# Up projection of a hybrid decoder layer: seven products in three PSUM banks, pairs interleaved, one subtraction moved from POOL to VectorE

## Chip, cores and metric

One core of one Trainium2 chip. The metric is the device time of one execution in microseconds (us); the median of three runs of the kernel before is 2045.83 us (2045.69 to 2045.98). TensorE (PE) multiplies, VectorE (DVE), ScalarE (ACT) and GpSimd (POOL) work on tiles in SBUF and PSUM, SyncE (SP) issues the DMAs.

## What is computed

One decoder layer: two token mixers (a Mamba-2 branch and windowed attention), their gated sum, a layer norm, a convolutional feed-forward block and a second layer norm. The change lies in the feed-forward block, of which the reference is

```
def conv_ffn(h, w_up, conv_w, conv_b, w_down):
    u = causal_depthwise_conv(jnp.einsum('bsd,df->bsf', h, w_up), conv_w, conv_b)
    gate, val = jnp.split(u, 2, axis=-1)
    return jnp.einsum('bsf,fd->bsd', jax.nn.silu(gate) * val, w_down)
```

with 1024 positions, h of 1024 channels, 2816 gate channels and as many value channels, and three taps in the convolution. All is float32.

## The kernel before

A float32 product is made of three products of rounded parts: a tile is split into a high part (`hi`, rounded by ScalarE, L100) and a low part (`lo`, the difference, L101, on the engine that the caller names), and hi x hi, hi x lo and lo x hi are summed.

**The up projection.** It runs in 22 *pairs* f = 0 to 21; a pair is 128 gate channels and the 128 value channels that belong to them, for all 1024 positions. The pair is computed as a 2 x 2 block product by Winograd's scheme with seven instead of eight block products. The rows of the blocks are gate and value weights, their columns the two halves of the 1024 input channels: A11, A12 are the halves of the gate weights (`uraw`, with parts `uhi` and `ulo`, made in `pair_first`), A21, A22 those of the value weights (`raw1`). On the other side stand the transposed activations, B11, B21, B22 (with their parts `hh`, `hl`) and the combinations T1 to T4, which are made once. `pair_s` loads `raw1` (L747) and makes four combinations S1 to S4 of the weights (L751 to L754) on POOL, except for pair 0, where it is VectorE, and splits each into `sh` (ScalarE) and `sl` (POOL). `pair` splits A22 into `a22h` and `a22l`, the second on POOL too.

The products are p1 = A11 B11, p2 = A12 B21, p3 = S4 B22, p4 = A22 T4, p5 = S1 T1, p6 = S2 T2, p7 = S3 T3. `prod` (L719 to L726) makes one of them from 12 matmuls of 128 x 128 by 128 x 512 (L724), so a pair has 84 and the stage 1848. Every product has a PSUM bank of its own: `bank` hands out six with the tag "b" and two with the tag "h".

`pair` then puts the four quarters of the result together on VectorE: cg (gate) has p1 + p2 in its first half, cv (value) and the second half of cg come from u2 = p1 + p6, u2 + p7, and p5, p4, p3. ScalarE copies p1 to SBUF (L903); VectorE does seven adds, each with one operand from SBUF and one from PSUM (L906, L907, L910, L912, L915, L916, L919). `gated` (L921) takes both through the convolution (`conv`: one ScalarE operation L126 and two VectorE steps L128 that read and write SBUF), applies silu (L122 on ScalarE, L123 on VectorE), multiplies (L926) and stores the result to DRAM (`asc`, L928). cg, cv, hg, hv and a scratch tile are five [128, 1024] tiles `cs` with one buffer each; `raw1` and S1 to S4 have one buffer each, `sh` and `sl` four.

**What sets the order.** A scheduler that simulates the program orders each engine's instructions; an engine then executes its list in order and waits on semaphores. Pairs 0 and 1 have p1 and p2 moved up into the layer norm ahead of the stage (NE and FR), and pair 0 its p3 (NP). Behind the stage, `load_d` loads the down weights (`draw`, split into `dh`, `dl`) and `load_a` the stored results (`ar`), for the down projection L982.

The functions that the diff touches, with what calls them:

Of the kernel before, what the change touches and what calls it, by code (L numbers as in the profile page):

```python
# [8 lines left out]
F32 = mybir.dt.float32  # L9
# [58 lines left out]
def hybrid(ctx: ExitStack, tc: tile.TileContext, xT, xn, win, wdt, wbr, wmix, wup, wdn,  # L68
# [634 lines left out]
    def bank(nm, tag="b"):  # L703
        return pb.tile([P, 512], F32, tag=tag, bufs=6 if tag == "b" else 2, name=nm)
# [15 lines left out]
    def prod(nm, a, b, tag="b"):  # L720
        p = bank(nm, tag)
        for k in range(4):
            for n, (w, x) in enumerate(((0, 0), (0, 1), (1, 0))):
                PE.matmul(p, a[w][:, k * P:(k + 1) * P], bop[b][x][:, k, :],  # L724
                          start=k == 0 and n == 0, stop=k == 3 and n == 2)
        return p  # L726

    pairs = {}
# [35 lines left out]
    with ExitStack() as ph2:  # L764
        tp = ph2.enter_context(tc.tile_pool(reuse_waits="tile", name="tp", bufs=2))
        lnt = []
        for i in (0, 1):
            lt = tp.tile([P, D], F32, bufs=1, name=f"lnt{i}") if i else onp.tile([P, D], F32, tag="on", name="lnt0")
            nc.sync.dma_start(lt, lnp[i].partition_broadcast(P))
            lnt.append(lt)  # L770

        last_t = [None]

        def transpose4(r, o, hs, ls, tag="h"):

# [24 lines left out]
        def tcols(v, t, tag="h"):  # L800
            h, l = bop[f"T{v}"]
            ts_ = slice(t * P, (t + 1) * P)
            transpose4(tsrc[v, t], 0, h[:, :, ts_], l[:, :, ts_], tag)

        for t in range(8):
            r = acc[t]
            nc.sync.dma_start(r, xn[t * P:(t + 1) * P, :])
            A.activation(r, r, AF.Copy, scale=ALPHA)
            p = [bank("pmix") for _ in range(2)]
            tq, ts_ = t // 4, slice((t % 4) * P, (t % 4 + 1) * P)  # L810
            for k in range(KT):
# [12 lines left out]
            if t == 7:  # L824
                bp_.close()
                yrp_.close()
                sp = sps.enter_context(tc.tile_pool(reuse_waits="tile", name="sp", bufs=1, side="right"))
                ttp = tts.enter_context(tc.tile_pool(reuse_waits="tile", name="ttp", bufs=1, side="right"))
                for nm in ("T4", "T2", "T3"):
                    bop[nm] = tuple(ttp.tile([P, 4, 512], F32R, name=f"{nm}{v}") for v in "hl")  # L830
                for t_, v in [(t_, v) for t_ in range(3) for v in (2, 3, 4)]:
                    tcols(v, t_, TT[(3 * t_ + v - 2) % len(TT)])

                for f_ in range(NE):
                    pair_first(f_)
# [44 lines left out]

    with ExitStack() as ph3:
        fp = ph3.enter_context(tc.tile_pool(reuse_waits="tile", name="fp", bufs=2))
        cs = [fp.tile([P, T], F32, bufs=1, name=f"cs{v}") for v in range(5)]

        def pair(f_):
# [5 lines left out]
            a22 = r["raw1"][:, 512:]  # L891
            r["A22"] = tuple(fp.tile([P, 512], F32R, tag=f"a22{v}", name=f"a22{v}") for v in "hl")
            split(a22, *r["A22"], G if EL[2] == "G" else V)
            cg, cv, hg, hv, t = cs
            lo_, hi_ = slice(0, 512), slice(512, 1024)
            u2 = fp.tile([P, 512], F32, tag="u2", name="u2")
            if f_ == NF - 1:

                p6, p7 = prod("p6", r["S2"], "T2"), prod("p7", r["S3"], "T3")
                p4 = prod("p4", r["A22"], "T4", "h")  # L900
            if "p1" not in r:
                pair_p12(f_)
            A.copy(cg[:, lo_], r["p1"])  # L903
# [3 lines left out]
            V.tensor_tensor(cg[:, lo_], cg[:, lo_], r["p2"], ALU.add)  # L907
            if f_ < NF - 1:
                p7 = prod("p7", r["S3"], "T3")
            V.tensor_tensor(cv[:, hi_], u2, p7, ALU.add)  # L910
            p5 = prod("p5", r["S1"], "T1")
            V.tensor_tensor(cg[:, hi_], u2, p5, ALU.add)  # L912
            if f_ < NF - 1:
                p4 = prod("p4", r["A22"], "T4", "h")
# [155 lines left out]
```

## Time and profile before

| what | us |
|---|---|
| median of three runs | 2045.83 |
| the profiled execution | 2044.2 |
| its span | 2042.2 |
| busy: TensorE | 1988.2 (97%) |
| busy: VectorE | 1342.6 (66%) |
| busy: POOL | 824.2 (40%) |
| busy: ScalarE | 687.5 (34%) |

The span is the time from the first to the last instruction of the profiled execution, and the execution's time lies 2.0 us above it. A share of busy time is a mean over the whole span, and says little of one stage. For a stage there is a table by windows (busy time of each engine, number of instructions in brackets, the granted clock of TensorE as PEclk, the DMA share), a timeline of one engine, a list of what ended the engine's waits, and the chain of waits that ended last, followed back from the end. In a timeline, `p<-hh,sl` is the matmul of a product whose operands are named; `idle before <-releaser` names the instruction that ended the wait. Matmuls overlap, so that one lasts 0.39 us while the next starts 0.23 us after it.

### The profile page before, as it was taken

To read this page: it belongs to the slowest core of one execution; us is meant where nothing else is said; L and a number is where in the kernel's file an instruction comes from. 1 tells how busy PE (TensorE), PEld (TensorE's weight loads), DVE (VectorE), ACT (ScalarE), POOL (GpSimd) and SP (SyncE) were. 2 spreads that over 40 slices of the span, in tenths; PEclk is the share of its full clock that TensorE was granted. 3 is DMA by queue.
4 is the path that set the end of the run, shared out by engine and by line. 5 is a ranking of instruction groups with operands and counts; after the bars stand their busy time and mean duration, and the time that the engine had idled before them with its cause. 6 is when DMAs were issued, how large, how long until landed. Compare 5 with 4: busy or idle time off the path is not lost.

```text
span 2042.2 us, 24586 instructions
## 1 busy us (share of the span) xinstructions
PE 1988.2 (97%) x9780; PEld 1615.5 (79%) x9780; DVE 1342.6 (66%) x1689; ACT 687.5 (34%) x899; POOL 824.2 (40%) x471
## 2 busy tenths in 40 slices
PE   8999999999999999999999998989999999999997
PEld 5888888888888888887888876867778787778886
DVE  6668567776356466764355378778888888863367
ACT  3334333333233333442311334143443334332122
POOL 1233233233231243441000044459999999700023
PEclk9999999999999999999999999999999999999999
DMA  4212212222222411114234344122222222265221
GB/s 159 75 62 93 94 52 102 84 73 99 108 93 104 122 61 57 51 70 158 93 104 145 134 155 155 46 68 73 83 77 79 93 72 83 73 218 164 88 87 62
DMA packets 82578, 197.50 MB, mean 97 GB/s; under 512 B 6496, under 2 KB 33696, under 8 KB 82464
## 3 DMA queue, kind: packets, MB, share of 16 engines
q1 hardware_dynamic: 76944, 191.14, 27.3%
q10 hardware_dynamic: 5520, 4.79, 0.9%
q8 instruction: 77, 1.26, 0.2%
q14 instruction: 37, 0.30, 0.0%
HBM read 153.82 MB, written 42.09 MB: 96 GB/s over the span
## 4 chain that ended last, share of the span: by engine, by line
PE 72%; POOL 14%; DVE 5%; DMA 4%; issue 3%; ACT 1%; SPq 0%; POOLq 0%; DVEq 0%; ACTq 0%
PE pd L183 33%; PE pbr L661 11%; PE pdn L982 11%; POOL sl L101 7%; PE p L724 4%; PE pmix L815 3%; POOL S L752 2%; POOL S L751 2%; POOL ulo L101 2%; PE yd L354 2%; PE psc L501 2%; PE yo L346 2%; PE pst L320 1%; POOL S L753 1%; PE py L540 1%
## 5 line engine op out<-in xcount | busy, mean ns | idle before, releaser
L183 PE MATMUL pd<-xl,whi_in 128*128 128x512 f32 x1056 | 338.0, 395 | 0.0
L183 PE MATMUL pd<-xh,wlo_in 128*128 128x512 f32 x1056 | 334.8, 394 | 0.0
L183 PE MATMUL pd<-xh,whi_in 128*128 128x512 f32 x1056 | 332.4, 393 | 0.3 <-DVE xs L128 0.3
L101 POOL TENSOR_TENSOR wlo_in<-wraw_in,whi_in 128x1024 fp32r<-128x1024 f32 x66 | 162.5, 2463 | 366.9 <-ACT whi_in L100 348.0
L183 PEld LDWEIGHTS pd<-xl,whi_in 128*128 128x128 f32 x1056 | 197.3, 188 | 43.5 <-issue 4.8
L183 PEld LDWEIGHTS pd<-xh,whi_in 128*128 128x128 f32 x1056 | 197.2, 188 | 43.2 <-issue 3.2
L183 PEld LDWEIGHTS pd<-xh,wlo_in 128*128 128x128 f32 x1056 | 197.2, 188 | 40.3 <-issue 2.1
L128 DVE SCALAR_TENSOR_TENSOR cs<-cs,colt,cs 128x1023 f32<-128x1023 f32 x88 | 173.8, 1978 | 35.5 <-ACT cs L126 34.0
L101 POOL TENSOR_TENSOR sl<-S,sh 128x512 fp32r<-128x512 f32 x88 | 184.0, 2105 | 0.1
L100 ACT CAST whi_in<-wraw_in 128x1024 fp32r<-128x1024 f32 x66 | 69.4, 1051 | 208.1 <-PE pd L183 127.8
L685 POOL TENSOR_TENSOR ba<-ba,bs 128x1024 f32<-128x1024 f32 x7 | 18.8, 2691 | 259.3 <-DVE ba L684 259.3
L661 PE MATMUL pbr<-yl,whi_br 128*128 128x512 f32 x384 | 117.9, 389 | 0.0
L661 PE MATMUL pbr<-yh,wlo_br 128*128 128x512 f32 x384 | 117.5, 389 | 0.0
L661 PE MATMUL pbr<-yh,whi_br 128*128 128x512 f32 x384 | 116.7, 389 | 0.0
L982 PE MATMUL pdn<-dh,ah 128*128 128x512 f32 x352 | 109.9, 390 | 1.4 <-ACT ah L100 1.4
L982 PE MATMUL pdn<-dl,ah 128*128 128x512 f32 x352 | 109.8, 390 | 1.4 <-POOL dl L101 0.9
L982 PE MATMUL pdn<-dh,al 128*128 128x512 f32 x352 | 110.0, 390 | 0.0
L584 POOL TENSOR_TENSOR out<-out,lnt 128x512 f32<-128x512 f32 x16 | 20.2, 1285 | 198.9 <-ACT out L583 198.9
L126 ACT ACTIVATE cs<-cs,colt 128x1024 f32<-128x1024 f32 x44 | 54.8, 1245 | 99.6 <-DMA asc<-cs 48.5
L661 PEld LDWEIGHTS pbr<-yh,wlo_br 128*128 128x128 f32 x384 | 72.1, 188 | 15.0
L661 PEld LDWEIGHTS pbr<-yl,whi_br 128*128 128x128 f32 x384 | 72.1, 188 | 15.0
L128 DVE SCALAR_TENSOR_TENSOR xs<-pd,colt,xs 128x1023 f32<-128x1023 f32 (+2 forms) x48 | 61.3, 1277 | 34.4 <-ACT xs L126 33.8
(271 smaller groups left out, 4266.8 us busy)
## 6 DMA issues: line engine op xcount, KB each, us to landing
wraw_in<-in_win SPq DMA_DIRECT2D x66, 512.0 KB, 3.5
m<-acd SPq DMA_DIRECT2D x32, 512.0 KB, 4.2
yraw<-ysc SPq DMA_DIRECT2D x24, 512.0 KB, 4.5
wraw_br<-in_wbr SPq DMA_DIRECT2D x24, 512.0 KB, 3.5
uraw<-in_wup SPq DMA_DIRECT2D x22, 512.0 KB, 4.4
raw<-in_wup SPq DMA_DIRECT2D x22, 512.0 KB, 3.4
asc<-cs SPq DMA_DIRECT2D x22, 512.0 KB, 5.3
draw<-in_wdn SPq DMA_DIRECT2D x22, 512.0 KB, 3.6
```

The costliest lines, as they stand in the source:

```text
L100: A.copy(hi, raw)
L101: (eng or V).tensor_tensor(lo, raw, f(hi), ALU.subtract)
L126: A.activation(h, p, AF.Identity, bias=col(c0 + taps), scale=col(c0 + taps - 1))
L128: V.scalar_tensor_tensor(h[:, s:], p[:, :T - s], col(c0 + taps - 1 - s), h[:, s:], ALU.mult, ALU.add)
L183: PE.matmul(p[:, q * 512:(q + 1) * 512], w[:, k * P:(k + 1) * P], x[:, q * 512:(q + 1) * 512], start=k == 0 and n == 0, stop=k == KT - 1 a ...
L346: PE.matmul(yo[:, j * P:(j + 1) * P], sts[j][:, i * P:(i + 1) * P], tcc[g][:, c * P:(c + 1) * P], start=True, stop=True)
L354: PE.matmul(yd[hh * 64:hh * 64 + 64, j * P:(j + 1) * P], xdts[j][:, i * P + hh * 64:i * P + hh * 64 + 64], m[:, hh, j * P:(j + 1) * P], st ...
L501: PE.matmul(psc[:, j * 256:(j + 1) * 256], qs[v][:, n * P:(n + 1) * P], kk[:, n0 * P:n0 * P + 256], start=w == 0, stop=w == 1)
L661: PE.matmul(p[:, q * 512:(q + 1) * 512], w[:, o:o + P], x[:, q * 512:(q + 1) * 512], start=k == 0 and n == 0, stop=k == 3 and n == 2)
L724: PE.matmul(p, a[w][:, k * P:(k + 1) * P], bop[b][x][:, k, :], start=k == 0 and n == 0, stop=k == 3 and n == 2)
L815: PE.matmul(p[q], x[tq][:, k, ts_], w[:, q * 512:(q + 1) * 512], start=k == 0 and n == 0, stop=k == KT - 1 and n == 2)
L982: PE.matmul(p[q], x[:, j], w[:, q * 512:(q + 1) * 512], start=j == 0 and n == 0, stop=j == nf - 1 and n == 2)
```

## The change

The seven products of a pair use three banks. `prod` gets an argument `onto`: the product is then accumulated onto a bank that already holds one.

- Bank pa: p1, copied to SBUF by ScalarE (L745, a new tile `p1` with two buffers), then p2 onto it; ScalarE copies the sum to cg's first half (L922).
- Bank pb: p6, then p7 onto it, then p4 onto that. VectorE reads it after each: u2 = p1 + p6 (L914), cv's second half = p1 + p6 + p7 (L924), cv's first half = p1 + p6 + p7 + p4 (L933).
- Bank pc (tag "h"): p5, then p3 onto it. VectorE adds it to cv's second half after p5 (L925), and with u2 into cg's second half after p3 (L936).

So VectorE has five adds a pair where there were seven (pair 0 has a sixth), and ScalarE two copies where there was one. `a22l` is made on VectorE. The pairs are interleaved: `head` of pair f (p1, p6, p5) comes ahead of `tail` of pair f - 1 (p4, p3), then comes `gated` of pair f - 1, then `mid` of pair f (p2, p7). The last pair has an order and banks of its own (`last`). cg and cv have two buffers. The room for this comes from the DMA scratch, which is set to 1024 bytes.

```diff
-    def pair_p12(f_, which=(1, 2)):
+    def prod(nm, a, b, tag="b", onto=None):
+        p = bank(nm, tag) if onto is None else onto
...
+                          start=onto is None and k == 0 and n == 0, stop=k == 3 and n == 2,
+                          skip_group_check=onto is not None)
+    def pair_p1(f_):
+        r = pairs[f_]
+        r["a"] = prod("pa", r["A11"], "B11")
+        r["p1"] = p1p.tile([P, 512], F32, tag="p1", name="p1")
+        A.copy(r["p1"], r["a"])
+    def pair_p2(f_):
+        prod("pa", pairs[f_]["A12"], "B21", onto=pairs[f_]["a"])
+        pairs[f_]["c11"] = True
...
-        cs = [fp.tile([P, T], F32, bufs=1, name=f"cs{v}") for v in range(5)]
+        hg, hv, t_ = (fp.tile([P, T], F32, bufs=1, name=f"cs{v}") for v in range(3))
...
+        def head(f_):
...
-            split(a22, *r["A22"], G if EL[2] == "G" else V)
+            split(r["raw1"][:, 512:], *r["A22"], V)
+            r["u2"] = fp.tile([P, 512], F32, tag="u2", name="u2")
+            r["cg"] = fp.tile([P, T], F32, tag="cg", name="cg")
+            r["cv"] = fp.tile([P, T], F32, tag="cv", name="cv")
...
+            if "a" not in r:
+                pair_p1(f_)
+            r["b"] = prod("pb", r["S2"], "T2")
+            V.tensor_tensor(r["u2"], r["p1"], r["b"], ALU.add)
+            r["c"] = prod("pc", r["S1"], "T1", "h")
+        def mid(f_):
...
+            if "c11" not in r:
+                pair_p2(f_)
+            A.copy(cg[:, lo_], r["a"])
+            prod("pb", r["S3"], "T3", onto=r["b"])
+            V.tensor_tensor(cv[:, hi_], r["p1"], r["b"], ALU.add)
+            V.tensor_tensor(cv[:, hi_], cv[:, hi_], r["c"], ALU.add)
+            if "p3" in r:
+                V.tensor_tensor(r["u2"], r["u2"], r["c"], ALU.add)
+        def tail(f_):
...
+            prod("pb", r["A22"], "T4", onto=r["b"])
+            V.tensor_tensor(cv[:, lo_], r["p1"], r["b"], ALU.add)
+            if "p3" not in r:
+                r["p3"] = prod("pc", r["S4"], "B22", onto=r["c"])
+            V.tensor_tensor(cg[:, hi_], r["u2"], r["p3"], ALU.add)
...
         for f_ in range(NF):
-            pair(f_)
-            if f_ < NF - 1:
-                gated(f_)
+            head(f_)
+            if f_:
+                tail(f_ - 1)
+                gated(f_ - 1)
+            (mid if f_ < NF - 1 else last)(f_)
...
-    nc = bacc.Bacc("TRN2", target_bir_lowering=False, num_devices=1)
+    nc = bacc.Bacc("TRN2", target_bir_lowering=False, num_devices=1, dynamic_dma_scratch_size=1024)
```

TensorE's order in the steady state, one period: p1 of pair f; p6 of f; 2 matmuls of p5 of f; 10 of p4 of f - 1; the other 10 of p5; the last 2 of p4; p3 of f - 1; p2 of f; p7 of f.

POOL, one pair in the middle of the stage (S_n: the combinations, told apart by their numbers; `uraw` and `raw` are the two weight tiles), before:

```order
311 L753 TENSOR_TENSOR S_11289<-uraw,raw_11285 128x512
312 L101 TENSOR_TENSOR sl<-S_11141,sh 128x512
313 L751 TENSOR_TENSOR S_11287<-raw_11285 128x512
314 L101 TENSOR_TENSOR a22l<-raw_11285,a22h 128x512
315 L752 TENSOR_TENSOR S_11288<-S_11287,uraw 128x512
316 L101 TENSOR_TENSOR sl<-S_11144,sh 128x512
317 L754 TENSOR_TENSOR S_11290<-uraw,S_11288 128x512
318 L101 TENSOR_TENSOR ulo<-uraw,uhi 128x1024
319 L101 TENSOR_TENSOR sl<-S_11288,sh 128x512
320 L101 TENSOR_TENSOR sl<-S_11289,sh 128x512
```

and with the change, where S1 to S4 have the lines L759 to L762:

```order
328 L761 TENSOR_TENSOR S_11670<-uraw,raw_11666 128x512
329 L101 TENSOR_TENSOR ulo<-uraw,uhi 128x1024
330 L101 TENSOR_TENSOR sl<-S_11524,sh 128x512
331 L759 TENSOR_TENSOR S_11668<-raw_11666 128x512
332 L760 TENSOR_TENSOR S_11669<-S_11668,uraw 128x512
333 L101 TENSOR_TENSOR sl<-S_11527,sh 128x512
334 L762 TENSOR_TENSOR S_11671<-uraw,S_11669 128x512
335 L101 TENSOR_TENSOR sl<-S_11669,sh 128x512
336 L101 TENSOR_TENSOR sl<-S_11670,sh 128x512
```

`a22l` is gone, nine operations are left, and `sl` of S2 and S3 of a pair are now followed by the next pair's S3 and `ulo`.

VectorE, one pair in the same place (`cs_10065` and `cs_10068` are hg, `cs_10066` and `cs_10069` hv, `p_...` a product's bank before and the copy of p1 after; silu, L123, stands right ahead of the first row), before:

```order
1264 L906 TENSOR_TENSOR u_11461<-cs_10063,p_11489 128x512
1265 L926 TENSOR_TENSOR cs_10065<-cs_10065,cs_10066 128x1024
1266 L907 TENSOR_TENSOR cs_10063<-cs_10063,p_11475 128x512
1267 L910 TENSOR_TENSOR cs_10064<-u_11461,p_11504 128x512
1268 L912 TENSOR_TENSOR cs_10063<-u_11461,p_11518 128x512
1269 L915 TENSOR_TENSOR cs_10064<-cs_10064,p_11532 128x512
1270 L916 TENSOR_TENSOR cs_10064<-cs_10064,p_11518 128x512
1271 L919 TENSOR_TENSOR cs_10063<-cs_10063,p_11547 128x512
1272 L128 SCALAR_TENSOR_TENSOR cs_10066<-cs_10064,colt,cs_10066 128x1023
1273 L128 SCALAR_TENSOR_TENSOR cs_10066<-cs_10064,colt,cs_10066 128x1022
1274 L128 SCALAR_TENSOR_TENSOR cs_10065<-cs_10063,colt,cs_10065 128x1023
1275 L128 SCALAR_TENSOR_TENSOR cs_10065<-cs_10063,colt,cs_10065 128x1022
```

and with the change:

```order
1317 L924 TENSOR_TENSOR cv<-p_12144,pb 128x512
1318 L925 TENSOR_TENSOR cv<-cv,pc 128x512
1319 L123 SCALAR_TENSOR_TENSOR cs_10068<-cs_10070,cs_10068 128x1024
1320 L960 TENSOR_TENSOR cs_10068<-cs_10068,cs_10069 128x1024
1321 L914 TENSOR_TENSOR u_12272<-p_12288,pb 128x512
1322 L933 TENSOR_TENSOR cv<-p_12144,pb 128x512
1323 L101 TENSOR_TENSOR a22l<-raw_12386,a22h 128x512
1324 L128 SCALAR_TENSOR_TENSOR cs_10069<-cv,colt,cs_10069 128x1023
1325 L936 TENSOR_TENSOR cg<-u_12128,pc 128x512
1326 L128 SCALAR_TENSOR_TENSOR cs_10069<-cv,colt,cs_10069 128x1022
1327 L128 SCALAR_TENSOR_TENSOR cs_10068<-cg,colt,cs_10068 128x1023
1328 L128 SCALAR_TENSOR_TENSOR cs_10068<-cg,colt,cs_10068 128x1022
```

The seven adds that stood together are now five that stand apart, among the operations of `gated`, and `a22l` stands between cv's add (L933) and the first conv step of hv.

## Rows read from the trace of the kernel before

**Rows 1.** The page, part 1: busy time and share of the span, instructions.

```profile
PE 1988.2 (97%) x9780; PEld 1615.5 (79%) x9780; DVE 1342.6 (66%) x1689; ACT 687.5 (34%) x899; POOL 824.2 (40%) x471
```

**Rows 2.** Chain of waits, 1330 to 1800 us: shares, then pieces (start, us, what).

```profile
by line: POOL sl L101 28.8%; PE p L724 17.7%; issue 11.1%; POOL S L752 7.5%; POOL S L751 7.4%; POOL ulo L101 7.4%; POOL S L753 4.8%; DMA asc<-cs 1.3%; DVE cs L128 1.3%; DVE dl L101 1.2%; DVE lnmv L591 0.9%; DMA ar<-asc 0.7%; DMA raw<-in_wup
...
1496.73 1.29 POOL S L753
...
1734.00 1.30 POOL S L753
```

**Rows 3.** Windows, matmuls of L724 alone: length, PE busy (count), PEclk, DMA share, GB/s.

```profile
1250.00:1352.00 102.00, 11.73 (x48) 0.99 0.21 82
1352.00:1408.50 56.50, 51.41 (x206) 0.93 0.18 60
1408.50:1438.00 29.50, 28.54 (x125) 1.00 0.33 108
1438.00:1480.00 42.00, 39.53 (x168) 0.96 0.24 75
1480.00:1787.50 307.50, 301.07 (x1307) 1.00 0.25 80
```

**Rows 4.** Windows: length, PE, PEld, DVE, ACT, POOL busy (count), PEclk, DMA, GB/s.

```profile
190.00:260.00 70.00, 70.00 (x367) 58.35 (x368) 45.53 (x58) 26.40 (x30) 15.26 (x7) 1.00 0.29 98
1480.00:1520.00 40.00, 39.34 (x173) 31.89 (x172) 33.21 (x27) 15.41 (x20) 39.53 (x21) 1.00 0.26 80
```

**Rows 5.** Timeline of TensorE in one pair: start, us, instruction [idle before <-releaser].

```profile
1508.26 0.50 PE L724 MATMUL p<-hh,sl 128*128 128x512 f32 x1 [0.40 <-POOL sl L101]
...
1510.66 0.39 PE L724 MATMUL p<-hh,uhi 128*128 128x512 f32 x1
...
1518.14 0.39 PE L724 MATMUL p<-T2h,sh 128*128 128x512 f32 x1
```

**Rows 6.** Timeline of POOL in one pair.

```profile
1497.98 2.26 POOL L101 TENSOR_TENSOR sl<-S,sh 128x512 fp32r<-128x512 f32 x1
...
1502.44 1.30 POOL L101 TENSOR_TENSOR a22l<-raw,a22h 128x512 fp32r<-128x512 f32 x1
1503.69 2.28 POOL L752 TENSOR_TENSOR S<-S,uraw 128x512 f32<-128x512 f32 x1
...
1508.29 1.30 POOL L754 TENSOR_TENSOR S<-uraw,S 128x512 f32<-128x512 f32 x1
```

**Rows 7.** Timeline of VectorE in the same pair.

```profile
1508.77 0.67 DVE L915 TENSOR_TENSOR cs<-cs,p 128x512 f32<-128x512 f32 x1
...
1511.48 3.79 DVE L128 SCALAR_TENSOR_TENSOR cs<-cs,colt,cs 128x1023 f32<-128x1023 f32 x2
```

**Rows 8.** Tile S: operations with ns min/median/max, first and last start.

```profile
L101 POOL TENSOR_TENSOR sl<-S,sh x88: 1262/2271/2296, 1341.7 to 1771.1; 128x512 fp32r<-128x512 f32 x88
...
L753 DVE TENSOR_TENSOR S<-uraw,raw x1: 676/676/676, 1333.5 to 1333.5; 128x512 f32<-128x512 f32 x1
...
L754 DVE TENSOR_TENSOR S<-uraw,S x1: 1545/1545/1545, 1339.0 to 1339.0; 128x512 f32<-128x512 f32 x1
```

**Rows 9.** Waits, 1330 to 1805 us: us in total, times, longest us.

```profile
PEld p L724 <- POOL sl L101: 17.8, 19, 2.9
```

**Rows 10.** Timeline of TensorE after a long wait in the stage's beginning.

```profile
1393.79 0.50 PE L724 MATMUL p<-T2h,sh 128*128 128x512 f32 x1 [2.01 <-ACT sh L100]
...
1395.31 0.63 PE L724 MATMUL p<-T3l,sh 128*128 128x512 f32 x1
1395.74 0.63 PE L724 MATMUL p<-hh,sh 128*128 128x512 f32 x1
```

**Rows 11.** Timeline of SyncE at the end of the stage.

```profile
1768.12 14.26 SPq L928 DMA_DIRECT2D asc<-cs  x2
1785.38 0.81 SPq L862 DMA_DIRECT2D draw<-in_wdn  x2
```

More of the change, by code (lines that the diff above doesn't have):

```diff
@@ L718, in hybrid @@
         bop[nm] = (hh_[q][:, o:o + 4], hl_[q][:, o:o + 4])
-    def prod(nm, a, b, tag="b"):
-        p = bank(nm, tag)
+    def prod(nm, a, b, tag="b", onto=None):
+        p = bank(nm, tag) if onto is None else onto
         for k in range(4):
@@ L724, in prod @@
                 PE.matmul(p, a[w][:, k * P:(k + 1) * P], bop[b][x][:, k, :],
-                          start=k == 0 and n == 0, stop=k == 3 and n == 2)
+                          start=onto is None and k == 0 and n == 0, stop=k == 3 and n == 2,
+                          skip_group_check=onto is not None)
         return p
@@ L736, in pair_first @@
         pairs[f] = dict(raw=raw, A11=(hi[:, :512], lo[:, :512]), A12=(hi[:, 512:], lo[:, 512:]))
-    def pair_p12(f_, which=(1, 2)):
+    def pair_p1(f_):
         r = pairs[f_]
-        for n in which:
-            r[f"p{n}"] = prod(f"p{n}", r[f"A1{n}"], f"B{n}1")
+        r["a"] = prod("pa", r["A11"], "B11")
[4 more added lines that the diff above has]
+        pairs[f_]["c11"] = True
     def pair_s(f_):
@@ L827, in hybrid @@
                 sp = sps.enter_context(tc.tile_pool(reuse_waits="tile", name="sp", bufs=1, side="right"))
+                p1p = sps.enter_context(tc.tile_pool(reuse_waits="tile", name="p1p", bufs=2, side="right"))
                 ttp = tts.enter_context(tc.tile_pool(reuse_waits="tile", name="ttp", bufs=1, side="right"))
@@ L835, in hybrid @@
                     pair_first(f_)
-                    for n in (1, 2):
-                        with tc.issue_after(last_t[0].ins) if 2 * f_ + n > FR else ExitStack():
-                            pair_p12(f_, (n,))
+                for n, (step, f_) in enumerate([(s_, f_) for s_ in (pair_p1, pair_p2) for f_ in range(NE)]):
+                    with tc.issue_after(last_t[0].ins) if n >= FR else ExitStack():
+                        step(f_)
                 pair_s(0)
@@ L882, in hybrid @@
         fp = ph3.enter_context(tc.tile_pool(reuse_waits="tile", name="fp", bufs=2))
-        cs = [fp.tile([P, T], F32, bufs=1, name=f"cs{v}") for v in range(5)]
-        def pair(f_):
+        hg, hv, t_ = (fp.tile([P, T], F32, bufs=1, name=f"cs{v}") for v in range(3))
+        lo_, hi_ = slice(0, 512), slice(512, 1024)
+        def head(f_):
             if f_ not in pairs:
@@ L890, in pair @@
                 pair_s(f_)
-            a22 = r["raw1"][:, 512:]
             r["A22"] = tuple(fp.tile([P, 512], F32R, tag=f"a22{v}", name=f"a22{v}") for v in "hl")
-            split(a22, *r["A22"], G if EL[2] == "G" else V)
-            cg, cv, hg, hv, t = cs
-            lo_, hi_ = slice(0, 512), slice(512, 1024)
-            u2 = fp.tile([P, 512], F32, tag="u2", name="u2")
+            split(r["raw1"][:, 512:], *r["A22"], V)
+            r["u2"] = fp.tile([P, 512], F32, tag="u2", name="u2")
@@ L897, in pair @@
+            r["cg"] = fp.tile([P, T], F32, tag="cg", name="cg")
+            r["cv"] = fp.tile([P, T], F32, tag="cv", name="cv")
             if f_ == NF - 1:
[L899 to L903, printed above, removed]
-            if f_ < NF - 1:
-                p6 = prod("p6", r["S2"], "T2")
-            V.tensor_tensor(u2, cg[:, lo_], p6, ALU.add)
@@ L907, in pair @@
[L907 to L914, printed above, removed]
-            V.tensor_tensor(cv[:, lo_], cv[:, hi_], p4, ALU.add)
-            V.tensor_tensor(cv[:, hi_], cv[:, hi_], p5, ALU.add)
@@ L917, in pair @@
-            if "p3" not in r:
-                pair_p3(f_)
-            V.tensor_tensor(cg[:, hi_], cg[:, hi_], r["p3"], ALU.add)
+                r["p6"], r["p7"] = prod("p6", r["S2"], "T2"), prod("p7", r["S3"], "T3")
+                return
+            if "a" not in r:
[5 more added lines that the diff above has]
+            r = pairs[f_]
+            cg, cv = r["cg"], r["cv"]
+            if "c11" not in r:
[6 more added lines that the diff above has]
+                V.tensor_tensor(r["u2"], r["u2"], r["c"], ALU.add)
@@ new lines, in tail, with last @@
+        def tail(f_):
+            r = pairs[f_]
+            cg, cv = r["cg"], r["cv"]
+            prod("pb", r["A22"], "T4", onto=r["b"])
[3 more added lines that the diff above has]
+            V.tensor_tensor(cg[:, hi_], r["u2"], r["p3"], ALU.add)
+        def last(f_):
+            r = pairs[f_]
+            cg, cv, u2 = r["cg"], r["cv"], r["u2"]
+            p4 = prod("p4", r["A22"], "T4", "h")
+            pair_p1(f_)
+            V.tensor_tensor(u2, r["p1"], r["p6"], ALU.add)
+            V.tensor_tensor(cv[:, hi_], u2, r["p7"], ALU.add)
+            c = prod("pc", r["S1"], "T1", "h")
+            V.tensor_tensor(cv[:, lo_], cv[:, hi_], p4, ALU.add)
+            pair_p2(f_)
+            A.copy(cg[:, lo_], r["a"])
+            V.tensor_tensor(cv[:, hi_], cv[:, hi_], c, ALU.add)
+            V.tensor_tensor(u2, u2, c, ALU.add)
+            p3 = prod("p3", r["S4"], "B22")
+            V.tensor_tensor(cg[:, hi_], u2, p3, ALU.add)
@@ L921, in gated @@
         def gated(f_):
-            cg, cv, hg, hv, t = cs
+            cg, cv = pairs[f_]["cg"], pairs[f_]["cv"]
             conv(cg, hg, C_FFN + 4 * f_, 3)
-            silu_half(hg, t)
+            silu_half(hg, t_)
             conv(cv, hv, C_FFN + 4 * (NF + f_), 3)
```

1 line of the change is left out of this document (removed).

## Prediction

> **What bounds the kernel now.** I read the page first, for the engine that is busiest: TensorE works 97% of the span [rows 1], so only stalls of its own, in one stage, can be worth anything here. Then the chain of waits over the up projection, 1330 to 1800 us: its largest item is not TensorE but the `sl` subtractions on POOL, 28.8%, with `S` and `ulo`, POOL too, behind them, and TensorE's products at 17.7% [rows 2]. The same rows give the period: the `S3` subtraction (L753) starts at 1496.73 and, twelve pairs later, at 1734.00, so a pair takes 237.27 / 12 = 19.77 us. Third, the table by windows: in a stretch of 40 us POOL is busy 39.53 us and VectorE 33.21 [rows 4].
>
> TensorE's own need comes from its timeline. From 1510.66 to 1518.14 us there are 33 steps of 0.2267 us with nothing between them; the row at 1508.26 shows the small wait on `sl` that comes once a pair [rows 5]. A pair has 84 matmuls: 84 x 0.2267 = 19.04 us. POOL's 19.77 us thus sets the pace and TensorE waits 0.73 us a pair; the list of waits has its weight load waiting for `sl` 19 times, 17.8 us in all [rows 9].
>
> The whole loss of the stage follows from the windows of L724 alone [rows 3]. With 0.2267 us for each counted matmul, 1352 to 1408.5 holds 206 (46.7 us of 56.5: lost 9.8); 1408.5 to 1438 holds 125 (lost 1.2); 1438 to 1480 holds 168 (lost 3.9); from 1480 to the last product at 1787.3 there are 1307 (296.3 of 307.3: lost 11.0, that is 15.5 pairs at 0.71). More than the last three, 16.1 us, cannot come back unless the start gets better too.
>
> **The change part by part.** *TensorE* issues the same 1848 matmuls; only their order and banks change. No term.
>
> *POOL* goes from ten operations a pair to nine: `a22l` leaves. From its start at 1502.44 to the next start at 1503.69 it takes 1.25 us, so POOL falls to 19.77 - 1.25 = 18.52 us, if its other operations stay as long as they are. They need not. A 512-wide POOL subtraction takes 1.30 us in some places (`S4`) and 2.26 to 2.28 in others (`sl`, `S2`) [rows 6]; over the stage `sl` goes from 1262 to 2296 ns with the median at 2271 [rows 8]. The long ones lie beside VectorE's operations that read two SBUF tiles (the two conv steps from 1511.48), the short `S4` beside its adds from PSUM, 0.67 each (the row at 1508.77) [rows 7]. So an SBUF operation on VectorE costs one POOL operation about 2.27 - 1.30 = 0.97 us, and six such a pair are there in both kernels. The `a22l` that arrives on VectorE is a seventh. Its own time is between 0.68 (`S3` done on VectorE alone) and 1.55 (`S4` there) [rows 8]; its cost to POOL is between 0 and 0.97, so POOL's loop is between 18.52 and 19.49. Since it works on 512 columns and the conv on 1023, about half, I take 0.5: 19.0 us, just under TensorE's 19.04. TensorE then sets the pace and the 11.0 us come back; at 19.49 it is (19.77 - 19.49) x 15.5 = 4.3.
>
> The Trainium skill, "SBUF — State Buffer", section "Who interferes with whom", says that a VectorE instruction with two SBUF inputs contends with a GpSimd instruction that reads SBUF, and that the loser waits for the whole instruction. By it `a22l` on VectorE would hold POOL up for its full 0.67 us and POOL's loop would be 19.2 us, longer than TensorE's; the rows agree that there is a cost, but 0.97 us beside a conv step is less than the step's whole length, so here half fits better.
>
> *VectorE* goes from seven adds of 0.67 to five and gains `a22l`: -1.35 + 0.68 to 1.55 us, so about nothing on 33.21 of 40 us busy [rows 4, 7]. What matters is the order, since the adds now free the banks. `p7` goes onto the bank that `u2` (L914) reads, `p4` onto the one that cv's add (L924) reads, `p3` onto the one that L925 reads. Each of these adds stands in VectorE's queue behind conv steps, silu and product of the pair before. Walking one period with the conv steps at the 1.9 us of [rows 7], L924 ends some 1.5 us before TensorE comes to `p4`, and `u2` is free some 1.2 us before `p7`: no term, but the cover is thin (the rival below).
>
> *ScalarE* copies `p1` as well, on an engine that is busy 15.41 of 40 us [rows 4]; `p2` follows it 48 matmuls later (10.9 us). The second `cg`/`cv` takes the conv of ScalarE off the reads of the pair after. No term. *SP*: `raw1` of the next pair now waits for VectorE's `a22l` instead of POOL's; by the walk it lands about 0.3 us before POOL wants it. No term.
>
> *The smaller DMA scratch* frees room and moves tiles: the first three `yraw` loads, their `rr` and three scalings (L637, L634, L639) are issued hundreds of us earlier, between 190 and 260 us. In SP's queue they stand among weight loads, behind stores that land well before them. TensorE is busy for all 70 us of 190 to 260 there and VectorE for 45.5 [rows 4], so three scalings and four loads beside it cost nothing; were the cover gone, it is below 1 us.
>
> *The start* gets dearer. Pairs 0 and 1 run before POOL has a lead, and the shared banks take away products that filled waits: in the walk TensorE waits 1.0 us for cv's add before `p4(0)`, 1.5 for `sh` of pair 1, 2.0 for `u2(1)` behind the conv of pair 0, 1.0 at pair 2 and 2.8 at pair 3. At 1408.5 us it has done 242 matmuls where the kernel before has done 48 + 206 = 254 (the 48 lie ahead of 1352): 12 x 0.2267 = +2.7 us. One more wait of 1.7 follows on `sl` of pair 3. And after long waits the clock falls: after the 2.01 us at 1393.79 matmuls come 0.43 us apart [rows 10], which is 1.2 GHz and not 2.4, and the granted clock of the window is 0.93 in the mean [rows 3]; some nine of them cost 9 x 0.2 = 1.8 us. Two of the new waits are as long, so 0 to 3.6, taken 1.7.
>
> *The end*. SP's queue is held for 14.26 us by a store of pair 20's result, so that the loads of the down weights come at 1785.38 [rows 11]. In the new order these loads stand ahead of it; a few small waits at the first down products shrink: 0 to -2, taken -0.5, against some 0.5 that pair 20's later gating may cost.
>
> **The sum**: -11.0 (steady) - 5.1 (1408.5 to 1480, the same cause) + 2.7 + 1.7 + 1.7 (start) - 0.5 (end) = -10.5 us. The profiled execution took 2044.2 us, 1.6 under the median of 2045.83; taken from the median the forecast is 2035.3 us. What a measurement here tells from no change is 0.2%, 4 us.
>
> **The rivals.** *POOL stays the bound*: an SBUF operation on VectorE costs POOL 0.97, whatever its length. POOL's loop is 19.4 to 19.49 and TensorE still waits on `sl` in every pair. -4.3 - 2.0 (the same share of 5.1) + 6.1 - 0.5 gives -0.7, and with 19.4 (-5.7 - 2.6) it is -2.7: 2043.1 to 2045.1, no change that can be told. For it: all six costs seen are near 0.97. Against: they are all beside operations twice as long. 0.15.
>
> *The lock holds for a whole instruction*: by [rows 6, 8] POOL's loop is 18.52 + 0.67 = 19.19, so of the 0.73 us 0.58 comes back: -9.0 instead of -11.0, 2037.3 us. The Trainium skill states this rule on the page cited above. 0.15.
>
> *Slower: VectorE's queue becomes the loop.* Through the shared bank TensorE's `p7` and `p4` wait for adds that stand behind operations of about 1.9 us [rows 7], and those operations wait for POOL. If VectorE's way from one `u2` to the next (busy 33.21 / 40 x 19.77 = 16.4 us a pair before [rows 4], now 15.7 to 16.6, and its waits on ScalarE and TensorE) is over 19.77, the pair is longer than before. At 20.5 us it is +0.73 x 15.5 = +11.3, with +6.1 from the start and -0.5, 2062.7 us. For it: the slack is only 1.2 to 1.5 us, and before the change six banks and the private products left TensorE free of this. Against: VectorE is busy 33.21 of 40 us with two adds more than after. 0.10.
>
> **How the numbers follow.** Forecast 0.60, rule of the lock 0.15, POOL the bound 0.15, VectorE the loop 0.10. Low end: all 16.1 us come back, the start costs nothing and the end gives 1: 2028.7, so 2029. High end: POOL at 19.4 with the dear start, 2044. Outside stay the slow rival and some hundredths on either side. Faster: 0.58 + 0.14 + 0.03 = 0.75; same: 0.02 + 0.01 + 0.10 = 0.13; slower: 0.10 + 0.02 = 0.12.
>
> **What would show it.** Right: between 1480 and the end of the products L724 starts every 0.2267 us without a wait per pair, POOL has idle time in each pair, and the period of `S3` is 19.0 to 19.1; the windows before 1420 hold fewer matmuls than before. Wrong: POOL still without idle time and waits of the weight load on `sl` 19 times (POOL the bound); waits of TensorE on VectorE's `u` or `cv` in every pair (the slow rival); `sl` beside `a22l` longer by the whole 0.7 (the lock).

## The result, and the profile after

The changed kernel takes 2031.55 us in the median of its runs (2030.26 to 2033.62) beside 2045.76 us of the kernel before: a ratio of 0.9931, 95% interval 0.9917 to 0.9946, or 14.2 us. The two profiled executions are 2044.2 and 2031.75 us, 12.45 apart; the rest is the 1.6 us by which the profiled execution of before lay under its median and the 0.2 us by which that of after lay above its own. In a second series the ratio was 0.9931 again (0.9919 to 0.9943).

The matmuls of the products alone, in the same windows as [rows 3] (length, PE busy, count, PEclk, DMA share, GB/s), kernel after:

```profile
1352.00:1408.50 56.50, 49.28 (x198) 0.94 0.21 72
1408.50:1438.00 29.50, 28.35 (x125) 1.00 0.22 76
1438.00:1480.00 42.00, 39.77 (x169) 0.96 0.23 83
1480.00:1787.50 307.50, 297.65 (x1314) 1.00 0.24 89
```

and all engines in the middle of the stage, to be held against [rows 4] (columns as there):

```profile
1480.00:1520.00 40.00, 40.00 (x179) 33.11 (x178) 33.22 (x25) 18.21 (x24) 35.55 (x20) 1.00 0.24 90
```

From 1480 us to the end of the products TensorE does not wait at all (40.00 of 40, 179 matmuls where there were 173), and POOL, which had 39.53 us of work in 40, has 35.55. The bound has gone over to TensorE. The last matmul of the products begins at 1777.26 us instead of 1787.04. The first S3 of this stretch and the one twelve pairs later, in POOL's timeline:

```profile
1484.06 1.35 POOL L761 TENSOR_TENSOR S<-uraw,raw 128x512 f32<-128x512 f32 x1 [0.89 <-PE pa L725]
...
1713.14 1.30 POOL L761 TENSOR_TENSOR S<-uraw,raw 128x512 f32<-128x512 f32 x1 [1.03 <-DMA raw<-in_wup]
```

A pair thus takes 229.08 / 12 = 19.09 us by POOL, and S3 waits 0.85 to 1.03 us in each of them. On TensorE p6 begins every 19.04 us.

What TensorE still waits for stands at the start of the stage. Every row of its timeline from 1360 to 1520 us that shows a wait, kernel after:

```profile
1369.08 0.47 PE L725 MATMUL pb<-T4h,a22h 128*128 128x512 f32 x1 [0.87 <-DVE cv L924]
...
1373.07 0.50 PE L725 MATMUL pb<-T2h,sh 128*128 128x512 f32 x1 [0.99 <-ACT sh L100]
...
1386.36 0.50 PE L725 MATMUL pb<-T3h,sh 128*128 128x512 f32 x1 [2.11 <-DVE u L914]
...
1390.87 0.50 PE L725 MATMUL pb<-T2h,sh 128*128 128x512 f32 x1 [1.45 <-ACT sh L100]
...
1433.22 0.50 PE L725 MATMUL pc<-hh,sl 128*128 128x512 f32 x1 [1.15 <-POOL sl L101]
...
1453.20 0.50 PE L725 MATMUL pc<-hh,sl 128*128 128x512 f32 x1 [2.23 <-POOL sl L101]
```

Behind the stage, windows of the down products (L982, now L1018) from the last product on, before and then after (length, PE busy, count, PEclk, DMA share, GB/s):

```profile
1787.30:1830.00 42.70, 39.86 (x170) 1.00 0.66 229
```

```profile
1777.50:1820.00 42.50, 41.32 (x180) 1.00 0.70 232
```

Ten matmuls more in the first 42.5 us: 2.3 us gained after the stage. The store of pair 20's result no longer holds SP's queue ([rows 11]: 14.26 us); of the four waits before (0.52, 0.92, 0.58 and 0.82 us) two are left, 0.25 and 0.93.

So the 12.3 us between the two spans are: 9.9 in the stage (from the last wait on the layer norm at 1350.56 and 1350.71 to the last product's end at 1787.27 and 1777.49), 2.5 behind it, and -0.15 ahead of it.

### The profile page after: what moved, and what is told of

Its sections match the earlier page's. It is cut to its first block, busy times and chain, and to the rows that moved or that the text cites. A ratio compares the mean times of both kernels' runs of the same rounds, so it can differ in the third digit from the quotient of the medians.

```text
span 2029.9 us, 24479 instructions
## 1 busy us (share of the span) xinstructions
PE 1982.7 (98%) x9780; PEld 1617.7 (80%) x9780; DVE 1337.6 (66%) x1669; ACT 705.3 (35%) x921; POOL 777.1 (38%) x449
## 4 chain that ended last, share of the span: by engine, by line
PE 77%; issue 14%; DVE 4%; POOL 3%; DMA 2%; ACT 1%; SPq 0%; DVEq 0%; ACTq 0%; POOLq 0%
PE pd L183 34%; PE pdn L1018 12%; PE pb L725 7%; PE pc L725 5%; PE pa L725 5%; PE pmix L823 3%; PE yd L354 2%; PE psc L501 2%; PE yo L346 2%; PE pst L320 1%; PE py L540 1%; PE ptp L526 1%; PE py L543 1%; PE px L311 1%; DMA bsc<-trow 1%
## 5 line engine op out<-in xcount | busy, mean ns | idle before, releaser
L101 POOL TENSOR_TENSOR sl<-S,sh 128x512 fp32r<-128x512 f32 x88 | 152.9, 1742 | 12.8 <-ACT sh L100 12.7
L1018 PE MATMUL pdn<-dh,ah 128*128 128x512 f32 x352 | 110.1, 390 | 0.9 <-ACT ah L100 0.9
L1018 PE MATMUL pdn<-dh,al 128*128 128x512 f32 x352 | 109.8, 390 | 0.2 <-DVE al L101 0.2
L1018 PE MATMUL pdn<-dl,ah 128*128 128x512 f32 x352 | 109.7, 389 | 0.0
L128 DVE SCALAR_TENSOR_TENSOR cs<-cg,colt,cs 128x1023 f32<-128x1023 f32 (+1 forms) x44 | 105.4, 2396 | 4.9 <-ACT cs L126 4.4
L100 ACT CAST sh<-S 128x512 fp32r<-128x512 f32 x88 | 54.0, 621 | 108.5 <-POOL S L760 71.3
L661 PEld LDWEIGHTS pbr<-yh,whi_br 128*128 128x128 f32 x384 | 72.1, 188 | 15.0
```

The lines of the kernel that those rows point to most:

```text
L128: V.scalar_tensor_tensor(h[:, s:], p[:, :T - s], col(c0 + taps - 1 - s), h[:, s:], ALU.mult, ALU.add)
L661: PE.matmul(p[:, q * 512:(q + 1) * 512], w[:, o:o + P], x[:, q * 512:(q + 1) * 512], start=k == 0 and n == 0, stop=k == 3 and n == 2)
L1018: PE.matmul(p[q], x[:, j], w[:, q * 512:(q + 1) * 512], start=j == 0 and n == 0, stop=j == nf - 1 and n == 2)
```

## The experiments

The change has two parts that could each be the cause: POOL's relief (`a22l` moved) and the new banks with the new order.

**1. `a22l` alone, in the kernel before.** The edit is

```diff
-EL = 'GGGG'
+EL = 'GGVG'
```

which makes L893 of the kernel before split A22 on VectorE.

> The kernel before with one thing changed: a22l is made on VectorE; banks and order are the old ones. Theory A (the gain is POOL's relief, wherever the adds stand): POOL's loop falls from 19.77 us to below 19.04, TensorE sets the pace from about 1480 us on, the products end 9 to 12 us earlier and the time is 2034 to 2037 us. Theory B (the relief works only with the shared banks and the interleaving, since VectorE with seven adds and a22l in a block becomes late): the period stays above 19.4 and the time above 2040 us.

Measured: ratio 0.9919 (0.9906 to 0.9933), 2028.21 us. The middle of the stage, and the first and last start of S3 on POOL (13 pairs apart):

```profile
1480.00:1520.00 40.00, 40.00 (x178) 33.15 (x177) 36.01 (x30) 14.90 (x20) 39.36 (x19) 1.00 0.22 79
```

```profile
1490.06 1.30 POOL L753 TENSOR_TENSOR S<-uraw,raw 128x512 f32<-128x512 f32 x1
...
1736.66 1.29 POOL L753 TENSOR_TENSOR S<-uraw,raw 128x512 f32<-128x512 f32 x1
```

TensorE is dense. POOL has next to no idle time and a loop of (1736.66 - 1490.06) / 13 = 18.97 us. TensorE's own period there is 19.04 us. The mechanism of theory A holds; the time came out 6 us under its range (4 in experiment 10), and the products end 15.8 us earlier and not 9 to 12, since the start lost less too: TensorE has no wait between 1394.34 and 1751.28 us.

**2. The rest of the change without `a22l`.**

```diff
-            split(r["raw1"][:, 512:], *r["A22"], V)
+            split(r["raw1"][:, 512:], *r["A22"], G)
```

> The changed kernel with a22l back on POOL: three banks, interleaving and five adds stay. Theory A (POOL's relief): POOL works about 17.5 us a pair in the changed kernel; with 1.3 to 2.3 us more it is at 18.8 to 19.8, most of the gain is lost, POOL has no idle time left, the time is 2038 to 2045 us. Theory B (banks and order are the gain): TensorE stays dense after 1480 us, time below 2034 us.

Measured: ratio 1.0027 (1.0017 to 1.0037), slower than the kernel before. TensorE waits for `sl` in each pair again, and a pair takes (1573.13 - 1492.82) / 4 = 20.08 us, 0.3 more than before the change. Timeline of POOL, the S3 operations of five pairs, with what they waited for:

```profile
1492.82 2.24 POOL L761 TENSOR_TENSOR S<-uraw,raw 128x512 f32<-128x512 f32 x1 [1.32 <-PE pb L725]
...
1512.98 2.14 POOL L761 TENSOR_TENSOR S<-uraw,raw 128x512 f32<-128x512 f32 x1 [1.42 <-DMA raw<-in_wup]
...
1532.94 2.25 POOL L761 TENSOR_TENSOR S<-uraw,raw 128x512 f32<-128x512 f32 x1 [1.31 <-DMA raw<-in_wup]
...
1552.89 2.37 POOL L761 TENSOR_TENSOR S<-uraw,raw 128x512 f32<-128x512 f32 x1 [1.19 <-PE pb L725]
...
1573.13 2.19 POOL L761 TENSOR_TENSOR S<-uraw,raw 128x512 f32<-128x512 f32 x1 [1.37 <-DMA raw<-in_wup]
```

Theory B is out. The gain is lost, as theory A says, but the time lies 5 us above its range, and POOL is not without idle time: it stands idle 1.2 to 1.4 us before each S3, for `raw1` or for TensorE's products on bank pb. With `a22l` on POOL the banks and the order give nothing in the stage, and make the pair longer (for want of a second `raw1`: experiment 6).

**3. The smaller DMA scratch alone**, in the kernel before:

```diff
-    nc = bacc.Bacc("TRN2", target_bir_lowering=False, num_devices=1)
+    nc = bacc.Bacc("TRN2", target_bir_lowering=False, num_devices=1, dynamic_dma_scratch_size=1024)
```

> The kernel before with the smaller DMA scratch alone, which moves tiles and lets three loads and scalings go hundreds of us earlier. Theory: these are hidden under TensorE, the time is that of the kernel before within 1 us. Rival: the moved tiles are part of the gain, 2 us or more faster than before.

Measured: ratio 1.000 (0.9991 to 1.0009). The moved loads cost and give nothing.

**4. Two buffers for `raw1`**, in the changed kernel:

```diff
-        raw1 = r["raw1"] = sp.tile([P, 1024], F32, name="raw1")
+        raw1 = r["raw1"] = sp.tile([P, 1024], F32, bufs=2, name="raw1")
```

> The changed kernel with two buffers for raw1. Theory: at the start of the stage POOL stands idle for 19 us until raw1 of pair 1 has come, since its only buffer is held by pair 0 until a22l; with a second buffer S1 to S4 of pair 1 are made in that time, the waits of TensorE for sh and sl (0.99, 1.45, 1.15 and 2.23 us) and the low clock after the last go, and it is 4 to 8 us faster than the changed kernel: 2024 to 2028 us. Rival: the start is held by VectorE (the wait of 2.11 us for u2 of pair 1) and by POOL's own loop, and the second buffer gives at most 2 us.

Measured: ratio 0.9896 (0.9883 to 0.9910), 2023.0 us, the fastest of all. POOL's timeline in the changed kernel, and in this one:

```profile
1346.83 2.34 POOL L101 TENSOR_TENSOR ulo<-uraw,uhi 128x1024 fp32r<-128x1024 f32 x1
1368.14 1.27 POOL L759 TENSOR_TENSOR S<-raw 128x512 f32<-128x512 f32 x1 [18.98 <-DMA raw<-in_wup]
```

```profile
1349.72 1.27 POOL L761 TENSOR_TENSOR S<-uraw,raw 128x512 f32<-128x512 f32 x1
1350.94 2.27 POOL L759 TENSOR_TENSOR S<-raw 128x512 f32<-128x512 f32 x1
1353.28 1.60 POOL L760 TENSOR_TENSOR S<-S,uraw 128x512 f32<-128x512 f32 x1
1354.96 1.60 POOL L762 TENSOR_TENSOR S<-uraw,S 128x512 f32<-128x512 f32 x1
1362.75 1.29 POOL L101 TENSOR_TENSOR sl<-S,sh 128x512 fp32r<-128x512 f32 x1 [6.20 <-ACT sh L100]
```

In the changed kernel POOL waits 18.98 us for `raw1` of pair 1; here it makes S1 to S4 of pair 1 in that time. The matmuls of the products in the first window and what TensorE waits for after 1400 us:

```profile
1352.00:1408.50 56.50, 52.16 (x219) 0.94 0.24 84
```

```profile
1424.96 0.50 PE L725 MATMUL pb<-T4h,a22h 128*128 128x512 f32 x1 [0.17 <-DVE cv L924]
...
1445.52 0.50 PE L725 MATMUL pc<-hh,sl 128*128 128x512 f32 x1 [0.55 <-POOL sl L101]
```

219 matmuls instead of 198, and of the waits for `u`, `sh` and `sl` listed above only 0.55 us is left, with 0.17 for cv, and the low clock does not come any more behind 1365 us. The wait for u2 of pair 1 went too; VectorE's order changed there as well (u2 now stands ahead of the conv steps), so which of the two took it away stays open. The theory holds, with the gain near its upper end (ratio of the two kernels 0.9896 / 0.9931 = 0.9965, 7 us) and the time 1 us under its range.

**5. The same with the old banks and the old order**: the kernel before with the edits of experiments 1, 3 and 4.

> The kernel before (its banks, its order) with a22l on VectorE, two buffers for raw1, and the small DMA scratch that makes the room. Theory A (shared banks and interleaving are not needed for the gain, they only shorten the first down products by 2 to 3 us and cost waits at the start): 1 to 3 us faster than a22l on VectorE alone, 2024 to 2028 us, within 4 us of the changed kernel with two raw1. Theory B (the second raw1 buffer pays only with the interleaved order): no faster than a22l on VectorE alone, 2028 us or more.

Measured: ratio 0.9904 (0.9891 to 0.9918), 2024.31 us. Theory B is out by the time, and the interval overlaps that of experiment 4, as theory A says. Against `a22l` alone the gain is 3 us by the ratio of experiment 1 and 5 by that of experiment 10, where theory A said 1 to 3; the intervals overlap, so the times alone do not show that the second buffer pays without the new order. The traces speak for it: TensorE's wait of 1.85 us for `sl` at 1394.34 us (experiment 1) does not come, and from the last wait on the layer norm to the last product's end it is 417.2 us, beside 420.2 and 419.1 with `a22l` alone.

**6. `a22l` on POOL again, with two `raw1`**: experiment 2 with the edit of experiment 4.

> The changed kernel with a22l back on POOL and two buffers for raw1. With one buffer the pair took 20.06 us though POOL stood idle 1.3 us in it, waiting for raw1 and for TensorE. Theory (raw1: its only buffer is held until POOL's a22l, which stands late in POOL's list, and the load of 3.3 us comes after): the idle time goes, POOL's 18.6 us of work fit under TensorE's 19.04, the stage is dense and the time is 2023 to 2028 us. Rival (POOL's amount of work with the contention: as in the kernel before, its loop is 19.5 or more as soon as it does not wait): 2034 to 2046 us.

Measured: ratio 0.9959 (0.9946 to 0.9971), 2035.95 us. S3 starts at 1480.38 and 13 pairs later at 1737.30, 19.76 us a pair, and POOL is full:

```profile
1520.00:1560.00 40.00, 39.17 (x172) 31.80 (x171) 31.13 (x23) 17.11 (x22) 39.37 (x21) 1.00 0.23 82
```

The rival holds. Without the wait for `raw1` POOL's ten operations take what they took before the change (19.77). The time is still under that of before because the start and the end are better (from the last wait on the layer norm to the last product's end it is 430.3 us beside 436.7, behind it 252.4 beside 254.9); the middle is not. So the 0.3 us a pair that experiment 2 lost go back to the one buffer of `raw1`.

**7. `a22l` twice**, to load VectorE further: in the kernel before with the edits of experiments 1 and 3,

```diff
+            more = fp.tile([P, 512], F32R, tag="more", bufs=1, name="more")
+            V.tensor_tensor(more, a22, f(r["A22"][0]), ALU.subtract)
```

> The kernel before with a22l on VectorE and made there twice, the second time into a tile that nobody reads (small DMA scratch for the room). It measures what one 512-wide VectorE subtraction of two SBUF tiles costs POOL, whose loop is 18.97 us a pair with one of them. Half (0.45 us, as POOL's operation beside a22l was longer): loop 19.4, TensorE waits 0.4 us a pair, 2034 to 2037 us. The rule of the whole instruction (0.7 us or more): 19.65 or more, 2039 us or more. No cost: dense, 2028 us.

Measured: ratio 1.0097 (1.0083 to 1.0111), 2064.13 us: slower than any theory said, and for another reason. The list of waits, 1330 to 1805 us (us in total, times, longest us), and one window:

```profile
ACT cs L122 <- DVE cs L128: 151.9, 21, 9.4
...
PEld p L724 <- ACT cs L905: 35.2, 18, 3.1
PE p L724 <- ACT cs L905: 27.7, 18, 2.7
```

```profile
1520.00:1560.00 40.00, 37.03 (x163) 30.00 (x161) 36.20 (x29) 14.54 (x20) 32.77 (x19) 1.00 0.22 79
```

TensorE waits for ScalarE's copy of p1 into cg (L905 here, L903 before). In ScalarE's queue this copy stands right behind silu (L122), which waits for VectorE's conv steps; POOL is at 32.77 of 40 and waits itself. VectorE's queue, with ScalarE's conv and silu between its steps, has become the loop, 20.83 us (waits of TensorE at 1474.50 and 1745.28, 13 pairs). So this run does not measure POOL's cost by its loop; by its rows it does (below).

**8. The same in the changed kernel.**

```diff
             split(r["raw1"][:, 512:], *r["A22"], V)
+            more = fp.tile([P, 512], F32R, tag="more", bufs=1, name="more")
+            V.tensor_tensor(more, r["raw1"][:, 512:], f(r["A22"][0]), ALU.subtract)
```

> The changed kernel with a22l made twice on VectorE, the second into a tile that nobody reads. In the old banks and order the same addition made VectorE's queue the loop: 20.83 us a pair, TensorE waiting for ScalarE's copy of p1 into cg, 2064 us. Theory A (the three banks, five adds and p1's own tile are worth room on VectorE, which shows only when VectorE is loaded): the pair stays at 19.04 to 19.2 us and the time at 2031 to 2035 us. Theory B (the adds that free the banks make TensorE at least as dependent on VectorE): TensorE waits in each pair on u or cv, 2045 us or more.

Measured: ratio 1.000 (0.9991 to 1.0008), 2044.68 us, above theory A's range and too near to theory B's 2045 to be told from it. S3 comes every 19.7 us in the mean (1489.67 to 1746.09, 13 pairs), with waits of TensorE for the add that frees bank pb (2.71 us once, and from 1480 us on 0.15 to 0.20 us five times) and for `sl` (1.2 us three times):

```profile
1456.29 0.50 PE L725 MATMUL pb<-T4h,a22h 128*128 128x512 f32 x1 [2.71 <-DVE cv L926]
...
1517.53 0.50 PE L725 MATMUL pc<-hh,sl 128*128 128x512 f32 x1 [1.20 <-POOL sl L101]
```

The loss from the second subtraction is 14 us here (beside the change in experiment 10, on the same chip) and 34 to 36 us in the old banks. So the new part does give VectorE room, though not enough for this, and one of the two waits is at the place that the slow rival named.

**9. One buffer each for cg and cv**, in the changed kernel: `bufs=1` in the two `fp.tile` lines of `head`.

> The changed kernel with one buffer each for cg and cv, as before the change. VectorE's order in the middle of the stage stays the same. Theory: VectorE's own order already keeps the adds behind the conv steps, so the second buffers buy nothing there: the changed kernel's time within 2 us. Rival: ScalarE's copy into cg waits for the conv steps, its queue holds the casts behind it and TensorE waits: 4 us or more slower than the changed kernel.

Measured: ratio 0.9935 (0.9921 to 0.9948), 2031.38 us. The theory holds; the second buffers buy nothing that shows.

**10. Change and `a22l` alone on one chip.**

> The changed kernel unaltered, beside a22l on VectorE alone on one chip, to tell whether the shared banks and the interleaving cost anything. Theory A (they cost waits at the start, 5 to 6 us, and give 2 to 3 back at the first down products): it is 2 to 4 us slower than a22l on VectorE alone. Theory B (the difference of the two first series was between the chips): equal within 1 us.

> The kernel before with a22l on VectorE alone, unaltered, beside the changed kernel on one chip. Theory A: 2 to 4 us faster than the changed kernel, its start without the waits for u, sh and sl of pairs 1 to 3. Theory B: equal within 1 us.

Measured: 0.9931 (0.9919 to 0.9943) for the change and 0.9929 (0.9917 to 0.9941) for `a22l` alone. Theory B holds for the time. The parts differ as theory A said: from the last wait on the layer norm (1349.88 and 1350.74) to the last product's end (1774.89 and 1769.86) the change is 5.9 us longer, and from there to the end of the span (2027.3 and 2026.3) 4.0 us shorter. The window of 1438 to 1480 us shows the start, change first:

```profile
1438.00:1480.00 42.00, 39.77 (x176) 32.62 (x175) 36.76 (x27) 17.65 (x24) 40.12 (x21) 1.00 0.25 93
```

```profile
1438.00:1480.00 42.00, 42.00 (x187) 34.80 (x186) 37.74 (x31) 14.90 (x20) 41.05 (x21) 1.00 0.24 83
```

## Why the prediction came out right

**What held.** The direction, the cause and the place. "TensorE then sets the pace and the 11.0 us come back": from 1480 us on nothing is lost, and S3 comes every 19.09 us, forecast 19.0 to 19.1. POOL's loop with `a22l` on VectorE was put at 19.0 us, "just under TensorE's 19.04"; in experiment 1, where POOL is full, it is 18.97. In the changed kernel itself POOL is not full: 35.55 of 40 us are some 17 us a pair, less than the lowest loop of the forecast (18.52), which had let the other operations keep their length; some `sl` take 1.75 us there (rows below) where 2.27 was the median [rows 8]. And S3 waits about 1 us a pair, in some pairs for `raw1` (the row at 1713.14), which the forecast had there 0.3 us before POOL wants it. Neither costs time while TensorE sets the pace. That the new banks and adds are no term in the steady state is shown by experiments 2, 6 and 10: with `a22l` back on POOL the gain of the middle is gone, with `a22l` alone it is all there. The DMA scratch is nothing (experiment 3).

**The start** was forecast term by term, and the first four waits are there: 0.87 for cv's add (forecast 1.0), 0.99 for `sh` of pair 1 (1.5), 2.11 for `u` of pair 1 (2.0), 1.45 at pair 2 (1.0). The 2.8 at pair 3 did not come: there is no wait between 1390.87 and 1433.22 us. Instead of one wait of 1.7 on `sl` of pair 3 there are two on `sl`, 1.15 and 2.23, in pairs 4 and 5 (p6 counted in TensorE's timeline). At 1408.5 us 48 + 198 = 246 matmuls were done, forecast 242. From there to the last product the loss was 17.4 us before (378.8 us for 1594 matmuls at 0.2267) and is 5.8 after (369.0 for 1602), so 11.6 came back where 16.1 - 3.4 = 12.7 was forecast. The low clock came once behind 1360 us, after the 2.23 us, where matmuls start 0.43 us apart (1.2 GHz):

```profile
1454.97 0.63 PE L725 MATMUL pc<-hl,sh 128*128 128x512 f32 x1
1455.39 0.63 PE L725 MATMUL pc<-hh,sl 128*128 128x512 f32 x1
```

After the 2.11 us they start 0.23 us apart. In the kernel before there were two such stretches, after 2.01 us [rows 10] and after 2.47. Each slows some seven matmuls by 0.2 us, so the term put at +1.7 came out near -1.4. In the second profile of the change (experiment 10) the low clock followed the wait of 2.12 us and not that of 2.23; what decides between the two stays open. The stage as a whole: forecast -10.0, measured -9.9. With terms that are 1 to 3 us off, a sum this near is luck: up to 1408.5 us four matmuls (0.9 us) fewer were lost than forecast, behind it 1.1 us less came back.

**What was off in size is the end**: "taken -0.5", measured -2.5. The step weighed 0 to -2 for the loads against "some 0.5 that pair 20's later gating may cost"; the gating cost nothing that shows, and the end gave more than the whole range. This term was mis-sized. From the last product's end to the end of the span it is 252.1 to 252.6 us in every profile with the new order (the change twice, experiments 2, 4, 6, 8 and 9) and 254.2 to 256.4 with the old one (before, experiments 1, 3, 5 and 7, `a22l` alone in 10). That it is SP's queue is read from the traces; no run took it alone. The other 1.8 us of the difference between 2035.3 and the median of 2031.55 are no step of the forecast: the profiled executions, on which it was made, differ by 12.45 us and not by 14.2.

**The rivals.** *POOL stays the bound* did not come, nor did the 19.19 us of *the lock holds for a whole instruction*: POOL's loop is 18.97 us in experiment 1, and 19.76 only with `a22l` on POOL (experiment 6). *VectorE's queue becomes the loop* did not come either, but it was near: one 512-wide operation more brings waits of TensorE that go back to VectorE in both bank layouts (experiments 7 and 8).

**The rule that I weighed wrongly.** I took the lock of the Trainium skill ("SBUF — State Buffer", section "Who interferes with whom") to cost POOL the full 0.67 us of `a22l`, and the row's 0.97 beside a conv step to speak against it. The changed kernel's rows agree with the rule, and not with my reading of it. Timelines of POOL and of VectorE in the changed kernel:

```profile
1611.48 1.30 POOL L762 TENSOR_TENSOR S<-uraw,S 128x512 f32<-128x512 f32 x1
1612.73 1.75 POOL L101 TENSOR_TENSOR sl<-S,sh 128x512 fp32r<-128x512 f32 x1
1614.96 1.75 POOL L101 TENSOR_TENSOR sl<-S,sh 128x512 fp32r<-128x512 f32 x1 [0.48 <-ACT sh L100]
```

```profile
1612.37 0.95 DVE L101 TENSOR_TENSOR a22l<-raw,a22h 128x512 fp32r<-128x512 f32 x1
1613.78 1.78 DVE L128 SCALAR_TENSOR_TENSOR cs<-cv,colt,cs 128x1023 f32<-128x1023 f32 x1 [0.45 <-ACT cs L126]
```

The ends come in turn: `S4` on POOL at 1612.78, `a22l` 0.54 later, `sl` 1.16 later, the conv step 1.08 later, the next `sl` 1.15 later. It looks as if only one of the two engines' instructions works at a time: each finishes a little less than its own undisturbed time (0.68, 1.30, and 1.27 for the shortest conv step of this kernel) after the other has finished. What POOL loses is the part of VectorE's instruction that is still to come when POOL's is ready: 0.45 us of 0.95 for `a22l`, some 0.97 of 1.27 for a conv step [rows 6]. It is the whole instruction that blocks, but here not the whole instruction that is lost. That the second of the two is blocked by a lock is what the Trainium skill states in that section, and the ends that come in turn, 0.54 to 1.16 us apart, agree.

POOL's loop in experiment 1 gives the same price, 18.97 - 18.52 = 0.45 us, where the forecast took 0.5, half of 0.97, for half the columns. That these are so near is luck: by the rows the loss goes by how much of VectorE's instruction is left when POOL's is ready. A second subtraction of the same width cost POOL 0.3 us in experiment 7 (last section).

## What to carry to other kernels

When one engine's loop is 0.7 us longer than TensorE's in each of 15 periods, the gain in these periods is bounded by that difference (11.0 us here), and one operation moved off that engine can be the whole of a large rewrite's effect: run the one-line move alone. Between POOL and VectorE, an operation that moves still takes a turn at what the two share; here it paid because it is shorter on VectorE (0.54 us of a turn against 1.25 on POOL) and VectorE had room for it in its queue, which it had not for a second one (experiments 7 and 8). Ahead of a stage, look for the engine that stands idle for one buffer: a second `raw1` gave another 7 us with the new order.

## What the runs showed that I had not expected

The turns of POOL and VectorE on instructions with two inputs from SBUF (ends 0.54, 1.16, 1.08 and 1.15 us apart in the rows above). In experiment 7 the second subtraction, in the middle of VectorE's adds, shows both sides of it, VectorE's rows first:

```profile
1604.75 0.76 DVE L101 TENSOR_TENSOR a22l<-raw,a22h 128x512 fp32r<-128x512 f32 x1
1605.43 1.77 DVE L895 TENSOR_TENSOR more<-raw,a22h 128x512 fp32r<-128x512 f32 x1
```

```profile
1604.92 1.74 POOL L101 TENSOR_TENSOR sl<-S,sh 128x512 fp32r<-128x512 f32 x1
1606.74 1.62 POOL L751 TENSOR_TENSOR S<-raw 128x512 f32<-128x512 f32 x1
```

`a22l` finds the way almost free (0.76 us against 0.67) and costs POOL's `sl` 0.44 (1.74 us against 1.30); `more` right behind it waits until POOL's `sl` has ended at 1606.66 and then takes 0.54 (1.77 in all); POOL's S1 then waits for `more` and takes 1.62 instead of 1.30. The second operation costs VectorE 1.1 us and POOL 0.3, and it was VectorE that had no room for it: how the cost is split depends on which engine comes second.
